# A hybrid diffusion layer on one core: four edits to the order of small steps (norm banks, down weights, output weights' low parts, state copy)

## The chip, the core and the metric

The kernel runs on one core of a Trainium2 chip: TensorE (PE) for matrix products into PSUM, VectorE (DVE), ScalarE (ACT) and GpSimd (POOL) for everything elementwise, SyncE (SP) for issuing most DMAs. Each engine works through its own instructions in order; semaphores tie them together. The metric is the device time of one execution in microseconds, the median of several.

## The reference

One layer over 1024 latent and 128 context tokens with d = 1024, in float32. Cut to what matters here:

```
h   = rmsnorm(x) * (1 + sc1) + sh1
o   = concat(diff_attention, RG-LRU, 2-D Fourier)(h @ w_in) @ w_out     # also new_k, new_v, new_h
x   = x + g1 * rmsnorm(o)
h   = rmsnorm(x) * (1 + sc2) + sh2
gt, up = split(h @ w_gate_up)                                            # hidden 2816
x   = x + g2 * rmsnorm((silu(gt) * up) @ w_down)
```

Attention has 4 heads, each with two score maps whose softmaxes are subtracted; a unit of work below is one head and one tile of 128 queries. new_h are the last states of the LRU.

## The kernel before

**Split products.** Every large product is made of three matmuls: each operand has a high part (fp32r, made by ScalarE) and a low part (operand minus high part, made by VectorE, `lo`, line 174). `mm3` (lines 184 to 186) issues them.

**Order.** The program is one hand-written sequence. Each engine executes its instructions in the order in which this sequence issues them. The LRU, rope, Fourier and modulation work is written as generators in queues; `tick` advances a modelled clock and lets each queue issue its next steps when the modelled time is due. `drain_lru` ticks until the four LRU queues are empty. The last steps of `lru_outs` transpose the four final states (`nht`), copy them (`lw<-nht`) and store them. The PSUM bank `nht` is the one that the next value tile takes.

**Attention.** The loop over n runs through 32 units (and 7 more steps to finish). Step n issues scores of unit n, transposes of unit n-3, products with the values of unit n-4, and the last transpose and scaling of unit n-6 (`finish_hi` on ScalarE, `finish_lo` on VectorE, which writes `mxl`). The softmax weights of unit n-1 are made by VectorE when n mod 3 = 0 and by GpSimd otherwise. The transposed weights have one PSUM bank, which `finish_lo` reads last in a step. Spread over these steps the output projection's weights are read from HBM in eight pieces (`load_wo`, two buffers `wor`), and their high (`woh`) and low parts (`wol`) are made in halves. The high parts are issued at n = 5, 7, 8, 10, 11, 13, ... (n mod 3 = 2 and 1), the low parts at n = 6, 7, 9, 10, 12, 13, ... (n mod 3 = 0 and 1).

**Output projection and second norm.** It runs over 9 token tiles. A finished tile is normed, transposed into two banks of the pool `dn` (`h2_turn`) and scaled (`h2_mod`, lines 1417 on ScalarE or 1420 on VectorE), and split into operands for the gate product. Tile 8 is transposed and scaled only after the gate products have begun.

**Gate products.** Seven products per weight visit g (Strassen-like, `PRODS`), numbered q; the operands of weight q are prepared four products ahead (`prep`). The first three visits use one token chunk only, while `second_chunk` prepares the operands of the other. Product results take PSUM banks in turn: number `nbank` modulo the length of the list `banks`, which has 4 entries, 6 from q = 4 on, and 8 after the transposed tile 8 has been taken. Entries 6 and 7 are the two banks of `dn`.

**Down projection.** 18 runs: column half n = 0 over the 9 tiles, then half n = 1 backwards. A run has 22 steps j of three matmuls. In the first run the down weights arrive: `load_d` reads 512 KB into one of three stages, `split_d(j + 10)` makes high and low part of one 512-column piece, and the second piece of a stage asks for the load three on. The hidden tile of a run is read back from HBM in two halves (`load_h`, two buffers `hr`) and split (`split_h`). `grow` copies a scale row to all partitions (`G2`); `post` uses it after each run.

Of the kernel before, what the change touches and what calls it, by code (L numbers as in the profile page):

```python
# [152 lines left out]
def _body(tc, nc, A):  # L153
# [465 lines left out]
    def lru_outs(f, lw, nh):  # L619
        for u in range(2):  # L620
            yield from until(("scan", u, 0), ("scan", u, 1))
            yield 2.021
            h, h1 = lru["scan", u, 0][0], lru["scan", u, 1][0]
            o = lru["scan", u, 1][1]
            POOL.tensor_tensor(h, h, h1, op=OP.add)
            yield 2.64
            for s0, o0, w in ((0, 0, NL), (NL + GAP, NL, NP)):
                DVE.tensor_tensor(o[:, o0:o0 + w], h[:, s0:s0 + w], ggr[u][:, o0:o0 + w],
                                  op=OP.mult)
            yield 0.994  # L630
            full = ([f.tile([P, TL], F32R, name=f"mo{i}", tag=i, bufs=2) for i in "ri"] if u else None)
            yield from store_mix(f, 4 + u, o, 4, full)
            lru["out", u] = True
        yield from until(*[("fin", u, d) for u in range(2) for d in range(2)])
        b = aux("nht", "a")
        PE.transpose(b[0:4, 0:P], nh.rearrange("p d u -> p (d u)"), ident)
        nhs = lw[0:4, 0, 0, 0]
        copy(ACT, nhs, b[0:4, 0:P])
        SP.dma_start(A["new_h"].rearrange("d (u p) -> (d u) p", p=P), nhs)
# [582 lines left out]
    for n in range(N + 7):  # L1222
        a, t_, v, c = n, n - 3, n - 4, n - 6
        if n == LEAD:
            play("v99")
            wp.release()
            hp.release()
            ax.release()
            wo = pool("wo")
            woh = wo.tile([P, KT, D], F32R, name="woh")  # L1230
            wol = wo.tile([P, KT, D], F32R, name="wol")
            mx = pool("mx")
            al = pool("al")
            tp = pool("tp", bufs=1, space=PSUM, side="right")
            G1 = mx.tile([P, D], F32, name="G1")
            ovec = mx.tile([P, NT, 4], F32, name="ovec")
            grow(G1, 0, 0)
        if n == N - 2:
            load_mix(0, ((4, KT), (0, 3)))
        if n == N + 1:  # L1240
            load_mix(0, ((3, 4),))
            load_x1in(0)
        if n == N:
            sc.release()
            dn = pool("dnps", bufs=2, space=PSUM)
            op = [pool(f"op{i}", space=PSUM) for i in range(2)]
        if has(a):
            U[a] = {}
            h, t = units[a]
            if t == 4 and h + 1 < NH:  # L1250
                load_head(h + 1)
            if t % 3 == 2 or t == 7:
                nx = 3 * h + t // 3 + 2
                if nx < 12:
                    load_q(nx // 3, nx % 3)
            if 3 <= n < 27 and n % 3 == 0:
                load_wo(n // 3 - 1)
            scores(a, 0)
            play(MID.get((n, 0), ""))
        on_dve = n % 3 == 0  # L1260
        if has(t_):
            tgroup(t_, 0, ACT)
        if has(v - 1):
            osquare(v - 1)
            oscale1(v - 1)
        if has(a):
            expo(a, 0)
        if 5 <= n < 29 and n % 3 != 0:
            split_wo((n - 5) // 3, 0 if n % 3 == 2 else 1)
        if has(v):  # L1270
            pv(v, 0)
        if N < n < N + 7:
            next(opg)
        if has(a):
            scores(a, 1, (0, 1))
            play(MID.get((n, 1), ""))
        if has(t_):
            tgroup(t_, 1, DVE)
        if 6 <= n < 30 and n % 3 != 2:
            split_wo_lo((n - 6) // 3, 0 if n % 3 == 0 else 1)  # L1280
        if has(n - 1):
            coef(n - 1)
            if not on_dve:
                weights(n - 1, POOL)
        if has(a):
            scores(a, 1, (1, 3))
            play(MID.get((n, 2), ""))
        if has(v):
            pv(v, 1)
        if has(t_):  # L1290
            bt = tgroup(t_, 2, ACT, c if has(c) else None)
        elif has(c):
            bt = tp.tile([P, 512], F32, name=f"tl{n}", tag="tp")
            PE.transpose(bt[:, CW:], U[c]["on"], ident)
        if has(c):
            finish_hi(c, bt[:, CW:])
        if has(v):
            pv(v, 2)
        if has(v):
            ocopy(v)  # L1300
        if N < n < N + 7:
            next(opg)
        if has(a):
            expo(a, 1)
        if has(c):
            finish_lo(c, bt[:, CW:])
        if has(v - 1):
            oscale2(v - 1)
        if has(n - 1) and on_dve:
            weights(n - 1, DVE)  # L1310
        if has(a) and units[a][1] == 6 and units[a][0] + 1 < NH:
            cache_hi(units[a][0] + 1)
        if has(a) and units[a][1] == 6 and units[a][0] + 1 < NH:
            cache_lo(units[a][0] + 1)
# [92 lines left out]
    def h2_mod(t, q):  # L1407

        r = 0 if t < 8 else 1
        if q == 0:  # L1410
            hu[t] = mo.tile([P, 4, 4, 64], F32, name=f"ou{t}", tag="ou", bufs=2)
        u, b = hu[t], hb.pop((t, q))
        for i in range(4):
            k = 4 * q + i
            o, x = u[:, 2 * q:2 * q + 2, i], b[:, i * P:(i + 1) * P].rearrange("p (h c) -> p h c", h=2)
            if t == 8 or q == HQ:
                ACT.activation(o, x, AF.Identity, scale=S2[:, r, k:k + 1],  # L1417
                               bias=M[:, r, 24 + k:25 + k])
            else:
                DVE.tensor_scalar(o, x, S2[:, r, k:k + 1], M[:, r, 24 + k:25 + k],  # L1420
                                  op0=OP.mult, op1=OP.add)
# [188 lines left out]
    H8 = 4  # L1610
    for v, (g, cs) in enumerate(VIS):
        last = v == NV_ - 1
        for c_ in ([(c,) for c in cs] if last else [cs]):
            if last and c_ == (1,):
                avp.release()
                dp = pool("dp", side="right", reuse_waits="tile")
                load_h(0, 0)
                G2 = [dp.tile([P, D], F32, name="G2"), raw[0][:, 1]]
                fv = dp.tile([P, NT, 2], F32, name="fv")
            for p in range(7):  # L1620
                q = 7 * v + p
                while nprep <= q + LEADQ:
                    prep(nprep)
                    nprep += 1
                if q == 4:
                    op[0].release()
                    gb = pool("gb", space=PSUM, reuse_waits="tile")
                    banks += [4, 5]
                bs = [product(q, c) for c in c_]
                if q in (H8, H8 + 1):  # L1630
                    h2_turn(8, q - H8)
                    h2_mod(8, q - H8)
                if q == H8 + 1:
                    banks += [6, 7]
                after(q, c_, bs)
                if extra is not None and next(extra, 1):
                    extra = None
                if v == NV_ - 2 and p == 3:
                    load_d(0)
                    load_d(1)  # L1640
                if last and c_ == (0,):
                    if p == 0:
                        dw += [mo.tile([P, 2, 512], F32R, name=f"dw{i}", tag="tm" if i < 2 else "ou",
                                       bufs=2) for i in range(4)] + slots
                    if p == 3:
                        load_d(2)
                    if 1 <= p <= 4:
                        split_d(p - 1)
                elif last:
                    if p == 1:  # L1650
                        load_h(0, 1)
                    if p == 4:
                        split_h(0, 0)
                    if p > 0:
                        split_d(p + 3)
# [30 lines left out]
    for i, (n, t) in enumerate(runs):  # L1686
# [6 lines left out]
        for j in range(NJ):  # L1693
            if i == 0 and j + 10 < NJ:
                split_d(j + 10)
            if j == 0:
                if i == 0:
                    grow(G2[0], 1, 0)
                    grow(G2[1], 1, 1)
                if nxt is not None:  # L1700
                    load_h(nxt, 0)
                    load_h(nxt, 1)
                if n:
                    load_x1(t)
            if i == 0 and j == 2:
                split_h(0, 1)
            if nxt is not None and j in ((14, 18) if i == 0 else (8, 14)):
                split_h(nxt, int(j > 8 if i else j > 14))
            if j == 1 and done is not None:
# [40 lines left out]
```

## Time and profile before

| | |
|---|---|
| three runs | 1446.28, 1448.0, 1450.58 us; median 1448.0 |
| profiled execution | 1453.06 us, its span 1451.3 us |
| TensorE busy | 1383.9 us, 95% of the span |
| VectorE, ScalarE, GpSimd busy | 822.7, 572.3, 426.6 us |
| stages in the span, about | scores and values 362 to 545, output projection to 656, gate products to 1160, down projection to the end |

Busy TensorE time contains matmuls whose ends are modelled. A row of waits names the waiting instruction by its engine, output and line and then the instruction that ended the wait. In names, the tile on the left of the arrow is written.

### The profile page before, as it was taken

The page shows a single profiled execution, that of the slowest core. Times are in us where ns is not written, and L with a number is a line of the kernel's source. Part 1 is how long each engine was busy: PE and PEld are TensorE (multiplying, and loading weights), DVE is VectorE, ACT ScalarE, POOL GpSimd, SP SyncE. Part 2 cuts the span into 40 slices and gives each one's busy share as a digit, 9 for nine tenths or more (in the row PEclk, how much of TensorE's full clock was granted, in tenths as well). Part 3 has the DMA queues.
Part 4 walks back from the last instruction along what each step waited for, and adds up shares of the span by engine and source line. Part 5 has one row for each costly group of instructions (what it writes and reads, how often), then busy time and mean ns, then how long its engine had stood idle before and what let it go on. Part 6 is the DMA issues. An engine that isn't in the chain of part 4 may idle for free.

```text
span 1451.3 us, 22745 instructions
## 1 busy us (share of the span) xinstructions
PE 1383.9 (95%) x8918; PEld 1256.6 (87%) x8918; DVE 822.7 (57%) x1251; ACT 572.3 (39%) x1134; POOL 426.6 (29%) x426
## 2 busy tenths in 40 slices
PE   7899999998998899998999999999999989999998
PEld 6787789897888888888899999999999968888886
DVE  5624454664777763676876767667666652233322
ACT  6511236734777773545422323323222342232111
POOL 2301111222565561446643423343324000000000
PEclk9999999999999999999999999999999999999999
DMA  8467750147744425562321322212222472324541
GB/s 311 148 238 257 254 178 30 62 159 169 171 122 121 116 68 175 174 216 101 116 68 71 99 75 92 82 62 85 73 91 78 137 270 82 106 99 172 181 160 58
DMA packets 108326, 193.39 MB, mean 133 GB/s; under 512 B 7702, under 2 KB 77755, under 8 KB 104763
## 3 DMA queue, kind: packets, MB, share of 16 engines
q1 hardware_dynamic: 108074, 191.41, 41.0%
q8 instruction: 70, 1.15, 0.3%
q10 hardware_dynamic: 144, 0.52, 0.1%
q14 instruction: 38, 0.30, 0.1%
HBM read 146.67 MB, written 45.24 MB: 132 GB/s over the span
## 4 chain that ended last, share of the span: by engine, by line
PE 51%; DMA 1%; DVE 1%; ACT 1%; POOL 0%; issue 0%; SPq 0%; DVEq 0%; POOLq 0%; ACTq 0%
PE g L184 11%; PE g L186 11%; PE g L185 11%; PE d L184 6%; PE d L185 6%; PE d L186 6%; DMA raw_gu<-in_w_down 1%; DMA hr<-HB 0%; DVE gu L174 0%; ACT gu L168 0%; DVE hd L174 0%; DVE dw L174 0%; POOL t L1353 0%; ACT ou L1417 0%; ACT hd L168 0%
## 5 line engine op out<-in xcount | busy, mean ns | idle before, releaser
L184 PE MATMUL g<-av,gu 128*128 128x320 f32 (+1 forms) x1232 | 365.6, 297 | 5.5 <-ACT ou L1417 5.5
L186 PE MATMUL g<-av,gu 128*128 128x320 f32 (+1 forms) x1232 | 364.9, 296 | 3.2 <-DVE gu L174 3.2
L185 PE MATMUL g<-av,gu 128*128 128x320 f32 (+1 forms) x1232 | 364.7, 296 | 0.0
L184 PEld LDWEIGHTS g<-av,gu 128*128 128x128 f32 x1232 | 233.4, 189 | 5.7 <-ACT ou L1417 5.7
L186 PEld LDWEIGHTS g<-av,gu 128*128 128x128 f32 x1232 | 233.5, 190 | 3.8 <-DVE gu L174 3.7
L185 PEld LDWEIGHTS g<-av,gu 128*128 128x128 f32 x1232 | 233.7, 190 | 0.0
L174 DVE TENSOR_TENSOR gu<-raw_gu,gu 128x512 fp32r<-128x512 f32 x139 | 141.1, 1022 | 40.1 <-ACT gu L168 40.1
L184 PE MATMUL pu<-hl,w 128*128 128x384 f32 x336 | 124.0, 369 | 4.6 <-POOL hl L174 3.8
L186 PE MATMUL pu<-hh,w 128*128 128x384 f32 x336 | 114.5, 341 | 0.0
L185 PE MATMUL pu<-hh,w 128*128 128x384 f32 x336 | 114.4, 341 | 0.0
L184 PE MATMUL d<-dw,hd 128*128 128x512 f32 x270 | 107.6, 399 | 6.8 <-DVE dw L174 6.8
L185 PE MATMUL d<-dw,hd 128*128 128x512 f32 x270 | 107.3, 398 | 0.0
L186 PE MATMUL d<-dw,hd 128*128 128x512 f32 x270 | 107.2, 397 | 0.0
L1370 POOL TENSOR_TENSOR raw_gu<-raw_gu,t 128x512 f32<-128x512 f32 x25 | 33.2, 1327 | 233.9 <-DVE gu L174 233.9
L939 PE MATMUL s<-ks,qs 128*128 128x384 f32 x384 | 91.6, 360 | 4.3 <-DMA ks<-KL 2.4
L1529 DVE TENSOR_TENSOR u<-g,u 128x320 f32<-128x320 f32 (+1 forms) x176 | 77.4, 450 | 29.8 <-PE g L186 29.8
L952 ACT ACTIVATE p<-s,nm 128x1152 f32<-128x1152 f32 x64 | 78.3, 1224 | 39.0 <-DVE nm L945 28.4
L945 DVE TENSOR_REDUCE nm<-s 128x1 f32<-128x1152 f32 x64 | 86.5, 1352 | 7.6 <-PE s L939 7.3
L1671 ACT ACTIVATE t<-d 128x512 f32<-128x512 f32 x18 | 10.7, 597 | 189.6 <-PE d L186 189.6
L168 ACT ACTIVATE gu<-raw_gu 128x512 fp32r<-128x512 f32 x139 | 83.4, 620 | 3.3 <-DMA raw_gu<-in_w_down 1.7
L1079 POOL TENSOR_SCALAR fv<-fv 128x1 f32<-128x1 f32 x9 | 2.7, 300 | 275.8 <-ACT t L1671 275.8
L184 PEld LDWEIGHTS pu<-hl,w 128*128 128x128 f32 x336 | 64.3, 191 | 21.6 <-issue 14.0
(276 smaller groups left out, 2868.8 us busy)
## 6 DMA issues: line engine op xcount, KB each, us to landing
raw_gu<-in_w_gu SPq DMA_DIRECT2D x25, 1024.0 KB, 4.8
hr<-HB SPq DMA_DIRECT2D x32, 704.0 KB, 4.7
wmb<-in_w_mod SPq DMA_DIRECT2D x32, 512.0 KB, 5.0
raw_gu<-in_w_down SPq DMA_DIRECT2D x22, 512.0 KB, 4.4
HB<-hf SPq DMA_DIRECT2D x18, 576.0 KB, 3.1
x<-in_x SPq DMA_DIRECT2D x18, 512.0 KB, 4.8
wm<-in_w_mod SPq DMA_DIRECT2D x16, 512.0 KB, 8.6
raw<-in_w_in_u SPq DMA_DIRECT2D x14, 512.0 KB, 7.7
```

The lines of the kernel that those rows point to most:

```text
L168: ACT.activation(out, in_, AF.Copy)
L174: eng.tensor_tensor(out, x, hi.bitcast(F32), op=OP.subtract)
L184: PE.matmul(out, wh, xl, start=first, stop=False)
L185: PE.matmul(out, wh, xh, start=False, stop=False)
L186: PE.matmul(out, wl, xh, start=False, stop=last)
L939: PE.matmul(b[:, j, :CW], q[:, st_, m, i * P:(i + 1) * P], ks[:, m, j * CW:(j + 1) * CW], start=(st_ == 0), stop=(st_ == 1))
L945: DVE.tensor_reduce(nm, s, axis=AX.XY, op=OP.max, negate=True)
L952: ACT.activation(p.rearrange("p (n c) -> p n c", c=CW), s, AF.Exp, bias=nm, accum_out=ss)
L1079: POOL.tensor_scalar(v[:, 0:1], v[:, 0:1], v[:, 1:2], D * EPS, op0=OP.add, op1=OP.add)
L1370: POOL.tensor_tensor(b21, b21, t2, op=OP.subtract)
L1529: add = lambda out, x: DVE.tensor_tensor(out, b, x, op=OP.add)
L1671: ACT.activation(t2, b, AF.Square, accum_out=fv[:, t, n:n + 1])
```

## The change

Five places move; none adds or removes work. (1) In `lru_outs` the state transpose is followed by a modelled delay of 4 us before the copy and the store. (2) Low parts of the output weights are issued one step later: at n = 7, 8, 10, 11, ... (n mod 3 = 1 and 2). (3) All eight scalings of tile 7 in `h2_mod` go to ScalarE (so far four of them to VectorE). (4) The list of banks gets its entries 6 and 7 at q = 13 and no longer at q = 5. (5) In the first run of the down projection the two scale rows are issued at step 11 and no longer at step 0, the next run's hidden halves at steps 6 and 8 and no longer at step 0.

```diff
@@ lru_outs
         PE.transpose(b[0:4, 0:P], nh.rearrange("p d u -> p (d u)"), ident)
+        yield 4.0
         nhs = lw[0:4, 0, 0, 0]
@@ attention loop
-        if 6 <= n < 30 and n % 3 != 2:
-            split_wo_lo((n - 6) // 3, 0 if n % 3 == 0 else 1)
+        if 7 <= n < 31 and n % 3 != 0:
+            split_wo_lo((n - 7) // 3, 0 if n % 3 == 1 else 1)
@@ h2_mod
-            if t == 8 or q == HQ:
+            if t > 6 or q == HQ:
@@ gate products
-                if q == H8 + 1:
+                if q == 13:
                     banks += [6, 7]
@@ down projection
             if j == 0:
-                if i == 0:
-                    grow(G2[0], 1, 0)
-                    grow(G2[1], 1, 1)
-                if nxt is not None:
+                if nxt is not None and i:
                     load_h(nxt, 0)
                     load_h(nxt, 1)
                 if n:
                     load_x1(t)
             if i == 0 and j == 2:
                 split_h(0, 1)
+            if i == 0 and j in (6, 8):
+                load_h(nxt, int(j > 6))
+            if i == 0 and j == 11:
+                grow(G2[0], 1, 0)
+                grow(G2[1], 1, 1)
```

## Rows read from the trace of the kernel before

**Rows 1.** Waits of TensorE: waiter, releaser: us in total, times, longest.

```profile
PE t L978 <- DVE mxl L1039: 11.0, 11, 1.6
PE d L184 <- DVE dw L174: 6.8, 2, 6.3
...
PE g L184 <- ACT ou L1417: 5.5, 1, 5.5
...
PE v L184 <- ACT lw L168: 3.2, 1, 3.2
PE g L186 <- DVE gu L174: 3.2, 2, 3.0
```

**Rows 2.** Waits of VectorE in the attention stretch, 370 to 545 us.

```profile
DVE wol L174 <- ACT woh L168: 11.5, 8, 1.4
```

**Rows 3.** Timeline of VectorE, attention: start, us, instruction, [idle before, releaser].

```profile
461.43 0.69 DVE L174 TENSOR_TENSOR wol<-wor,woh 128x512 fp32r<-128x512 f32 x1 [1.43 <-ACT woh L168]
...
463.63 0.34 DVE L1039 SCALAR_TENSOR_TENSOR mxl<-t,gsub,mxh 128x128 fp32r<-128x128 f32 x1
...
466.37 0.56 DVE L170 COPY th<-t 128x384 f32<-128x384 f32 x1 [1.13 <-PE t L978]
...
479.25 0.69 DVE L174 TENSOR_TENSOR wol<-wor,woh 128x512 fp32r<-128x512 f32 x1 [1.43 <-ACT woh L168]
```

**Rows 4.** Timeline of TensorE, attention.

```profile
464.03 0.55 PE L978 MATMUL t<-ident,wt 128*128 128x128 f32 x3 [1.18 <-DVE mxl L1039]
```

**Rows 5.** Timeline of ScalarE, attention.

```profile
466.61 1.22 ACT L952 ACTIVATE p<-s,nm 128x1152 f32<-128x1152 f32 x1 [0.59 <-POOL wt L971]
```

**Rows 6.** Timeline of VectorE, first gate products.

```profile
673.22 1.75 DVE L174 TENSOR_TENSOR gu<-t,gu 128x512 fp32r<-128x512 f32 x1
...
699.54 3.44 DVE L174 TENSOR_TENSOR gu<-raw_gu,gu 128x512 fp32r<-128x512 f32 x2
```

**Rows 7.** Timeline of SyncE: value tiles and states, then output weights.

```profile
318.94 0.90 SPq L877 DMA_DIRECT2D VS<-nk  x2
...
320.93 0.31 SPq L639 DMA_DIRECT2D out_new_h<-lw  x1
...
487.83 0.54 SPq L914 DMA_DIRECT2D wor<-in_w_out  x1
```

**Rows 8.** Timeline of ScalarE, last norm and first gate products.

```profile
659.74 0.63 ACT L1097 ACTIVATE tm<-x 128x512 f32<-128x512 f32 x1 [0.89 <-DVE x L1096]
...
672.25 0.63 ACT L168 ACTIVATE gu<-t 128x512 fp32r<-128x512 f32 x1 [1.45 <-POOL t L1353]
672.78 1.49 ACT L1417 ACTIVATE ou<-ot,M,S 128x128 f32<-128x128 f32 x4
```

**Rows 9.** Windows: us; busy us (instructions) by engine; granted clock, DMA share, GB/s.

```profile
671.74:678.56 6.82, 4.24 (x16) 4.24 (x17) 5.76 (x7) 5.70 (x15) 4.73 (x4) 0.50 0.01 2
...
1176.92:1183.70 6.78, 5.26 (x12) 4.13 (x13) 5.51 (x8) 5.98 (x8) 0.00 (x0) 0.50 0.62 213
```

**Rows 10.** Timeline of SyncE, first down run.

```profile
1164.74 0.44 SPq L1065 DMA_DIRECT2D G<-GR  x1
...
1165.70 2.28 SPq L1600 DMA_DIRECT2D hr<-HB  x2
1168.02 13.77 SPq L1585 DMA_DIRECT2D raw_gu<-in_w_down  x6
```

**Rows 11.** Single DMA issues at 1160.8 and 1168.0: KB, us to landing.

```profile
raw_gu<-in_w_down SPq DMA_DIRECT2D x1, 512.0 KB, 3.3
...
raw_gu<-in_w_down SPq DMA_DIRECT2D x1, 512.0 KB, 9.0
```

**Rows 12.** Timeline of VectorE, first down run.

```profile
1164.81 1.29 DVE L174 TENSOR_TENSOR dw<-raw_gu,dw 128x512 fp32r<-128x512 f32 x2
1166.01 1.62 DVE L174 TENSOR_TENSOR hd<-hr,hd 128x1408 fp32r<-128x1408 f32 x1
```

**Rows 13.** DMA issues over the whole span: count, KB, median us to landing.

```profile
hr<-HB SPq DMA_DIRECT2D x32, 704.0 KB, 4.7
```

## The prediction

> **What bounds the kernel now.** The table above has TensorE busy for nearly the whole span, so I read first which waits of TensorE are left, and what stands behind each. The list of its waits has the longest single ones, and the largest sum, where three of the edits are [rows 1]: 11.0 us in eleven pieces for `mxl`, VectorE's low part of the attention output; 6.8 us in two pieces for a low part of down weights; one piece of 5.5 us for ScalarE's line 1417 (the last tile's second norm) ahead of gate product 6; one of 3.2 us for the copy of the LRU states. The last row, 3.2 us with one piece of 3.0 for a gate weight's low part, is touched by no edit and matters all the same. Then I read each place in the timelines of all engines, to see whether the wait is the bound there or only what happens to come last.
>
> **Low parts of the output weights.** In the units with n mod 3 = 1, VectorE is asked for the low part of the very half whose high part ScalarE makes in the same unit. It stands still for 1.43 us, eight times, 11.5 us in all [rows 2, 3]. Queued behind the waiting instruction are the unit's coefficient, its second row maximum and `mxl` (463.63), which frees the one bank for transposed weights; TensorE then begins its transposes at 464.03 after 1.18 us of waiting [rows 3, 4]. Eight such pieces, the longest of them 1.6, are 8 x 1.2 + 0.4 = 10.0 of the 11.0 us [rows 1].
> With the edit the low part in this unit is that of a half whose high part is two units old, and the other half's low part goes to the unit with n mod 3 = 2, a unit after its high part. The 1.43 us go; 0.69 us of work moves from n mod 3 = 0 to 2. What hides it there: VectorE idles 1.13 us before its copy at 466.37 in that unit, which comes earlier by the same shift [rows 3]. What is late next: ScalarE's exponential at 466.61 waits for GpSimd's weights [rows 5]; GpSimd begins these with the coefficient that stood behind the 1.43 us, so this moves forward with the rest. Gain 10.0 us. Bounds: 11.5, and 1.5 if the moved work is slowed.
> The subtraction of this shape takes 0.69 us here, and 1.75 us at 673.22, where GpSimd works beside it [rows 3, 6]. [...] I take 0.69, since the low part at 461.43 already lies in such a unit and takes 0.69.
>
> **The states' copy.** The 3.2 us for `lw` are real, but the edit only adds a delay to a list worked off by a modelled clock. On SyncE the store of the last value tile is the second at 318.94, and the states' store follows it at 320.93 [rows 7]: these steps are issued by the final draining loop, in which no other list has anything left. Four more ticks put no instruction between transpose and copy. Cost 0. Bounds, should something move: 3.2 us gained, or 4.0 (the modelled delay) lost.
>
> **The last norm and its banks.** Today product 6 goes to a bank that holds the transposed last tile, which ScalarE empties from 672.78 on (four instructions, 1.49 us); ScalarE had been held for 1.45 us by GpSimd's weight sum [rows 8]. With the edit product 6 has a bank long empty, and the wait of 5.5 us goes. But the products behind it need their weights' low parts, and these come from a chain in which TensorE has no part: high part on ScalarE, low part on VectorE, sums on GpSimd, and between them the second token chunk's operands. Product 8 needs the low part that starts at 673.22 and ends at 674.97; product 18 needs the first of the two that start at 699.54 (3.44 us for both), at about 701.3 [rows 6], and this is the piece of 3.0 us in [rows 1]. TensorE ends product 5 at 668.8 (678.56 less 4.24 us busy [rows 9] less 5.5). From there to product 18 are 12.3 products of twelve matmuls; at half clock 16 took 4.24 us, so 0.132 each at full clock, 1.6 us a product, 1.8 with some margin: 22 us of work in 32.5. Without the bank wait TensorE meets the weights' low parts earlier, waits in more and smaller pieces, and leaves at 701.3 as before. Gain 0. Under the same cover lies a new wait: with six banks until product 13 and eight after it, products 16 and 17 get the banks of 12 and 13, whose sums are late. The four norm instructions of tile 7 that go from VectorE to ScalarE are the 1.49 us of above; ScalarE's next one waits 0.89 us for VectorE anyway (659.74) [rows 8], so 0, at most 0.6.
> Bounds: 7.6 us gained (5.5, and 2.1 for 4.24 us at a granted clock of 0.50 [rows 9]), and 6 lost (rival D).
>
> **The first down tile.** The ninth of its eleven weight loads is asked for at 1168.02 and lands 9.0 us later; one with nothing in flight lands after 3.3 [rows 10, 11]. On SyncE it stands behind two scale rows (1164.74, each 512 KB) and two reloads of a hidden tile (1165.70, each 704 KB), the second of which waits for the low part that ends at 1166.01 + 1.62 [rows 10, 12]. Its own buffer was free at 1164.81 + 1.29 = 1166.1 [rows 12]. With the edit it leaves at 1166.1 with one weight load ahead: I take a landing at 1169.5 to 1171. From landing to matmul took 1.4 us (1177.0; 1183.70 less 5.26 busy [rows 9]). So it is ready at 1170.9 to 1172.4, and TensorE, without its first wait of 0.5, wants it at 1171.6. The last pieces follow at the pace of their low parts; I allow 1.1 us of waiting in all. Of 6.8 us of waits and 2.6 of half clock (5.26 us busy at 0.50 [rows 9]), together 9.4, 8.3 go.
> What is late next: the hidden tile with which the second run begins. Its reload now goes out behind the sixth step's load, by my estimate at 1170.2 (the eighth load lands at 1167.9, its high and low parts take 1.9). It lands 4.7 later by the page's median [rows 13], at 1174.9; a high and a low part of at most 1.62 each [rows 12] end at 1178.1. The second run wants it at 1171.6 + 6 x 0.7 + 1.1 = 1176.9. That gives back 1.2 us. The scale rows, asked for at about 1176, are needed only by the first run's norm, whose bank is not wanted for eight runs: 0. Gain 8.3 - 1.2 = 7.1. Bounds: 9.4, and 0.2 where the reload takes 9.0 us (5.5 of waiting and 2.6 of half clock).
>
> **Sum.** The profiled execution took 1453.1 us, 5.1 above the median: 1453.1 - 10.0 - 0 - 0 - 7.1 = 1436.0. From the median of 1448.0 it is 1430.9; I say 1431. Behind each of the places TensorE has no wait of this size left, so the gain should reach the end.
>
> **Rivals.**
> A. The bank wait is worth its price, since the weight chain shortens with it: 1431 - 7.6 = 1423. For it: it is the second longest wait. Against: no link of the chain waits for TensorE. 0.10.
> B. The low parts meet GpSimd, and 1.25 us a period shrink to 1.25 - 1.06 = 0.19: 1.5 us for eight, 1439.5. For it the 1.75 us at 673.22, against it the 0.69 at 461.43 [rows 3, 6]. 0.12.
> C. The reload takes the weight load's place as the late transfer: 0.2 gained there, 1438. For it the 9.0 us, against it that the scale rows now lie behind it. 0.10.
> D. The gate stretch, its idle time cut small, runs at the lower clock throughout: 12.3 x 12 x 0.265 = 39 us in place of 32.5, 1437. Half clock did follow the 5.5 us wait [rows 9]. [...] 0.04.
> E. Slower. A piece of output weights is asked for only when the low part of the piece two before has freed its buffer, and SyncE, which works in order, holds the loads of queries and heads behind that request. Now the buffer is free at 479.25 + 0.69 and the request leaves at 487.83 [rows 3, 7]: 7.9 us of slack, of which the edit uses one unit, 17.82 / 3 = 5.9 (461.43 to 479.25 are three units). Past 7.9 each us would count for six pieces; from a slip of 10.8 on the 17.1 us are undone. A slip of two units, 11.9: 1431 + 6 x 4.0 = 1455. 0.03.
> The forecast keeps 0.61, with a range of its own of 1426 to 1436.
>
> **Numbers.** 1422 to 1440 takes in the cases A to D. About 0.3%, 4.3 us, is what a measurement of this kernel can tell from no change. Slower than that: E and a little for mishaps, 0.04. Within it: B and C together, 0.06. Faster: 0.90.
>
> **What would show it.** Right: `wol` no longer waits for `woh`; TensorE's row for `mxl` falls from 11.0 to between 1 and 3 us; no wait for line 1417, but several smaller ones for gate low parts, with product 18 some 32 us behind product 5 as before; no 6.3 us wait in the first down tile, and one of about 1 us for `hd` ahead of the second; the 3.2 us at the states' copy unchanged. Wrong: low parts that take 1 us or more, a wait of ScalarE for `wor`, a second run that waits several us for `hd`, or product 18 well before 32 us.

## The result and the profile after

The changed kernel took 1432.6 us in the median of four runs (1430.3 to 1439.2) beside 1449.3 for the kernel before in the same comparison: a ratio of 0.9892, interval 0.985 to 0.9934, 15.7 us. Its profiled execution took 1430.3 us, with a span of 1428.5. Timed again later (the run "changed, again" below, with a profile of its own, here called the second profile) it took 1433.05 against 1452.14: 0.9869, 0.9852 to 0.9885, 19.0 us.

TensorE's waits after the change (waiter, releaser: us in total, times, longest), answering to [rows 1]:

```profile
PE g L186 <- DVE gu L174: 7.3, 6, 2.2
...
PE v L184 <- ACT lw L168: 3.5, 1, 3.5
PE d L184 <- DVE dw L174: 3.1, 2, 1.9
...
PE t L979 <- DVE mxl L1040: 1.1, 3, 0.6
...
PE d L186 <- DVE hd L174: 0.9, 1, 0.9
PE g L184 <- ACT av L168: 0.8, 1, 0.8
```

The row for `mxl` has fallen from 11.0 to 1.1, and that for line 1417 (5.5) is gone. In its place the gate's low parts have grown from 3.2 to 7.3 in six pieces. The wait at the states' copy is as it was. In the first down tile 6.8 us have become 3.1, and a new 0.9 for the hidden tile stands ahead of the second run.

VectorE in the attention after the change, answering to [rows 3]. These are the low parts in the units with n mod 3 = 1 of two successive periods of three units (start, us, instruction, [idle before]):

```profile
447.92 0.68 DVE L174 TENSOR_TENSOR wol<-wor,woh 128x512 fp32r<-128x512 f32 x1
...
464.16 0.68 DVE L174 TENSOR_TENSOR wol<-wor,woh 128x512 fp32r<-128x512 f32 x1
```

No idle time stands before them, and a period is 16.24 us long; before it was 17.82 [rows 3].

Where the time went, by stage. Each stage runs from its first matmul in TensorE's timeline to that of the next stage, the last one to the last matmul; us:

| kernel | ahead of the scores | attention | output projection | gate | down |
|---|---|---|---|---|---|
| before | 342.5 | 198.8 | 115.8 | 503.1 | 284.7 |
| changed | 338.2 | 185.1 | 115.8 | 502.8 | 280.1 |
| changed, again | 336.6 | 185.7 | 115.8 | 502.8 | 281.4 |
| low parts only | 343.4 | 185.1 | 115.8 | 503.1 | 284.2 |
| banks only | 342.7 | 197.5 | 115.8 | 503.1 | 285.0 |
| down only | 343.0 | 198.0 | 115.8 | 503.1 | 279.3 |
| scales only | 341.7 | 197.5 | 115.8 | 503.1 | 281.9 |
| reloads only | 342.0 | 197.8 | 115.8 | 504.1 | 280.8 |
| low parts apart | 344.4 | 185.8 | 115.8 | 504.1 | 279.3 |
| gate two thirds | 341.5 | 185.0 | 115.8 | 503.0 | 281.5 |
| fourth stage | 340.9 | 186.4 | 115.8 | 503.1 | 279.0 |
| no token sums | 341.4 | 186.0 | 115.8 | 502.3 | 279.5 |
| all three | 345.3 | 185.2 | 115.8 | 502.8 | 278.5 |
| apart and stage | 343.1 | 185.0 | 115.8 | 502.8 | 278.6 |

Rows with "only" are the kernel before with a part of the change, those below them the changed kernel with something more or less; each is one profile. The first column is to be read first. All kernels but "all three" have the same order of instructions up to the scores, and still it runs from 336.6 to 344.4. So the 4.3 us by which the two profiled executions differ there are no effect of the change. From the scores on, the changed kernel is 18.6 us shorter than the kernel before: 13.7 in the attention, 0.3 in the gate stage and 4.5 in the down stage; its second profile is 16.6 us shorter. Single profiles scatter by 1 to 2 us in the attention and in the down stage: the attention takes 197.5 to 198.8 us in the five profiles with the old order of low parts and 185.0 to 186.4 in the nine with a new one, 12.4 apart in the mean.

### The profile page after: what moved, and what is told of

Its sections match the earlier page's. It is cut to its first block, busy times and chain, and to the rows that moved or that the text cites. A ratio compares the mean times of both kernels' runs of the same rounds, so it can differ in the third digit from the quotient of the medians.

```text
span 1428.5 us, 22758 instructions
## 1 busy us (share of the span) xinstructions
PE 1375.9 (96%) x8918; PEld 1248.9 (87%) x8918; DVE 822.0 (58%) x1247; ACT 573.4 (40%) x1138; POOL 427.6 (30%) x426
## 4 chain that ended last, share of the span: by engine, by line
PE 49%; DVE 2%; issue 1%; ACT 1%; DMA 1%; POOL 0%; DVEq 0%; POOLq 0%; SPq 0%; ACTq 0%
PE g L186 10%; PE g L184 10%; PE g L185 10%; PE d L186 6%; PE d L184 6%; PE d L185 6%; DVE gu L174 1%; DMA hr<-HB 1%; DVE av L174 0%; ACT gu L168 0%; DMA raw_gu<-in_w_down 0%; DVE u L1530 0%; DVE hf L1530 0%; DVE hd L174 0%; ACT av L168 0%
## 5 line engine op out<-in xcount | busy, mean ns | idle before, releaser
L1672 ACT ACTIVATE t<-d 128x512 f32<-128x512 f32 x18 | 10.7, 596 | 186.4 <-PE d L186 186.4
```

The source lines that it names most:

```text
L1672: ACT.activation(t2, b, AF.Square, accum_out=fv[:, t, n:n + 1])
```

## The experiments

**The three parts alone.** Each is the kernel before with one part of the change, the lines as in the diff above: the low parts; the banks with the scalings of tile 7; the scale rows with the reloads.

> The kernel before with only the output weights' low parts one step later. By the prediction's term it is 10.0 us shorter than the kernel before. By the stage in the two traces, where the units with n mod 3 = 2 fell from 7.0 to 5.6 us from scores to scores and all 24 units from 362 on gained 13.7 us with 1.5 of it at unit 0 that the change doesn't touch, it is about 12 us shorter. If the gain of the attention came from elsewhere (a different clock, a shift in the transfers), it is less than 8. In the trace VectorE's wait of the low parts for the high parts (11.5 us in eight pieces) should be gone, and TensorE's wait for mxl 1 to 2 us.

> The kernel before with only the banks given to gate products from product 13 on and tile 7's scalings on ScalarE. My theory: the weights' low parts are the bound there, so no gain, within 2 us of the kernel before, the wait for ScalarE's line 1417 replaced by 6 to 8 us of waits for gate low parts, and product 18 again some 32 us behind product 5. Rival: the bank wait is worth its price and the whole gate stage is 5.5 to 7.6 us shorter.

> The kernel before with only the scale rows and hidden reloads of the first down run moved. By the prediction's term 7.1 us shorter; by the down stage of the two traces (284.3 against 279.7 us from the first matmul to the last) 4.5 us shorter, with waits of 3 us for down weights and 1 us for the hidden tile left. Rival: nothing (under 1 us), since the reload is late instead.

Beside 1451.7 us for the kernel before, the low parts alone took 1438.8 (ratio 0.9911, 0.9888 to 0.9934: 12.9 us), the banks alone 1451.9 (1.000, 0.9983 to 1.0016) and the down part alone 1445.8 (0.9959, 0.9941 to 0.9977: 6.0 us). The parts sum to 18.9 us, and the change as a whole measured 15.7 and 19.0. For the low parts the estimate from the stage (12) came nearer than the prediction's term (10.0), though the interval (9.6 to 16.3 us) holds both. The theory of no gain at the banks holds. The down part gave 5.4 us in the stage of its profile, between the two figures expected (7.1 and 4.5).

The gate stage is read from two rows of TensorE's timeline per kernel: the first gate matmul, and the first matmul of product 18 that uses its weight's low part. Before:

```profile
657.06 0.39 PE L184 MATMUL g<-av,gu 128*128 128x320 f32 x1
...
701.34 0.41 PE L186 MATMUL g<-av,gu 128*128 128x320 f32 x1 [2.97 <-DVE gu L174]
```

The kernel with the banks alone:

```profile
656.00 0.39 PE L184 MATMUL g<-av,gu 128*128 128x320 f32 x1
...
700.32 0.41 PE L186 MATMUL g<-av,gu 128*128 128x320 f32 x1 [2.21 <-DVE gu L174]
```

44.28 and 44.32 us. With the bank wait TensorE stood once for 5.5 us and once for 3.0; without it, it stands for 6.8 us in five pieces for low parts and reaches product 18 at the same distance. Of the fourteen profiles eight have 44.3 us here, and five, with the old banks and with the new, 45.2 to 45.3 (the one left has 45.0, below); what makes this difference of 1 us is open.

**The low parts apart.** The moved low parts also leave a unit in which VectorE makes the softmax weights (n mod 3 = 0). Was that a part of the gain?

```diff
-        if 7 <= n < 31 and n % 3 != 0:
-            split_wo_lo((n - 7) // 3, 0 if n % 3 == 1 else 1)
+        if 6 <= n < 30 and n % 3 == 0:
+            split_wo_lo((n - 6) // 3, 0)
+        if 8 <= n < 32 and n % 3 == 2:
+            split_wo_lo((n - 8) // 3, 1)
```

> The changed kernel, but each first half's low part back in the units with n mod 3 = 0, where it was before the change, and each second half's in the units with n mod 3 = 2. No low part then stands behind a high part of its own unit, and none lies in a unit with n mod 3 = 1. If the gain of the attention is the removed wait alone, the stage is as long as in the changed kernel (185 us from the first scores to the output projection, within 1). If a part of it came from work leaving the units in which VectorE also makes the softmax weights (n mod 3 = 0), the stage is 2 us or more longer than that.

The attention took 185.8 us against 185.1 and 185.7 in the two profiles of the changed kernel: the gain comes from the removed wait, and within 1 us it doesn't matter which of the other units takes the work. The kernel took 1431.2 us (0.9862, 0.9838 to 0.9886), which can't be told from the changed kernel.

**The two halves of the down part.**

> The kernel before with only the two scale rows of the first down run moved to step 11, the hidden reloads left at step 0. My theory is that both the rows and the reloads stand on SyncE ahead of the ninth weight load, and that the second reload's wait for its buffer is what holds the load back: the load then still leaves at about 2 us after its buffer is free, lands after 5 to 6 us in place of 9, and 2 to 4 us are gained. Rival: the two rows of 512 KB were all of it, and the gain is that of the whole part (4.5).

> The kernel before with only the hidden reloads of the first down run moved to steps 6 and 8, the scale rows left at step 0. By my theory the ninth load leaves on time but shares the transfers with 1 MB of scale rows: 2 to 4 us gained. Rival: the order on SyncE was all of it, and the gain is that of the whole part (4.5).

The scale rows alone gave 0.9978 (0.9961 to 0.9996), 3.2 us; the reloads alone 0.9969 (0.9949 to 0.9989), 4.5 us. By the stage it is 2.8 and 3.8, where both together have 5.4. The wait for weights in the first down run (6.8 before) is, in this order, with the scale rows moved, with the reloads moved, and with both:

```profile
PE d L184 <- DVE dw L174: 4.6, 1, 4.6
```

```profile
PE d L184 <- DVE dw L174: 3.7, 1, 3.7
```

```profile
PE d L184 <- DVE dw L174: 2.1, 2, 1.5
```

Each half does part of it and neither all, so both theories hold and both rivals fall. The ninth weight load, on SyncE and by its landing, shows what each does. Before, it leaves 7.9 us after the first down matmul and lands 9.0 us later. With the scale rows moved it leaves at 7.9 as before and takes 6.5; with the reloads moved it leaves at 5.4 and takes 8.5; with both, 5.1 and 6.2. So the reloads hold the request back on SyncE, and the scale rows, under way with it, lengthen its landing.

**Is TensorE the bound in the gate stretch?** One matmul in three is left out of products 6 to 17:

```diff
+            if 6 <= q < 18:
+                PE.matmul(b, w[:, 0, ks], al_[:, a, k, :n], start=k == 0, stop=False)
+                PE.matmul(b, w[:, 1, ks], ah[:, a, k, :n], start=False, stop=k == 3)
+                continue
             mm3(b, w[:, 0, ks], w[:, 1, ks], ah[:, a, k, :n], al_[:, a, k, :n], k == 0, k == 3)
```

> The changed kernel with one of three matmuls (high part by high part) left out of gate products 6 to 17, so the result is another. TensorE then has some 6 us less to do between product 5 and product 18. If the chain of weights is the bound there, product 18 still comes some 32 us behind product 5, TensorE's waits in that stretch grow by 5 to 6 us, and the kernel is within 1.5 us of the changed kernel. If TensorE itself is the bound behind its bank waits, product 18 comes 5 to 6 us earlier and the kernel is that much shorter.

The same two rows of this kernel:

```profile
642.33 0.39 PE L184 MATMUL g<-av,gu 128*128 128x320 f32 x1
...
687.53 0.42 PE L186 MATMUL g<-av,gu 128*128 128x320 f32 x1 [1.57 <-DVE gu L174]
```

45.20 us: with a third of its matmuls gone TensorE is no earlier, and the stage is as long as ever (503.0). The kernel took 1435.0 us in one run. The chain of weights is the bound here, shown. One expectation was missed: TensorE's waits in the stretch grew from 8.0 to 10.8 us and not by 5 to 6. The granted clock was 0.85 there, where the two profiles of the changed kernel have 1.00 and 0.96, so TensorE was busy for 34.2 us where it had been for 36 to 37.

**What is the chain bound by?** The token sums of `second_chunk` are left out:

```diff
             token_operands1(AV[1], hu[t], t - PT[0])
-            token_sums(hu[t])
             yield
```

> The changed kernel without GpSimd's token sums for the second token chunk (lines 1390 to 1393, four sums for each of four tiles, left out, so the result is another). So far product 18 came 44.3 us after the first gate product whatever the banks did. My theory is that VectorE's chain of low parts is the bound there and that GpSimd working beside it stretches the low parts (1.04 us in the mean for 128x512 from SBUF, in place of 0.69). Without the sums the low parts should average under 0.95 us, and product 18 should come 3 to 7 us earlier. Rival: the chain is bound by its order or by GpSimd's weight sums alone, and product 18 still comes within 1 us of 44.3.

VectorE's costliest group from 640 to 690 us (busy us, mean ns | idle before), first in the changed kernel, then in this one:

```profile
L174 DVE TENSOR_TENSOR gu<-raw_gu,gu 128x512 fp32r<-128x512 f32 x14 | 14.4, 1041 | 4.5 <-ACT gu L168 4.5
```

```profile
L174 DVE TENSOR_TENSOR gu<-raw_gu,gu 128x512 fp32r<-128x512 f32 x13 | 13.0, 1013 | 3.4 <-ACT gu L168 3.4
```

The low parts still take 1.01 us in the mean, and product 18 comes at 688.18 - 643.21 = 44.97 us. My theory falls: without these sums the chain is no shorter. But the mean mixes two kinds of low part. In the changed kernel sixteen low parts of weights begin between the first product and product 18. Those that began more than 0.1 us into a sum of GpSimd took 0.83 to 1.77 us, and each ended about 0.55 us after that sum. The others took 0.68 to 0.69, but for one of 1.26 that began within 0.1 us of a sum's start; another such took 0.68. Without the token sums GpSimd makes its weight sums earlier, and these do the same to a low part at the start of the stage. GpSimd and VectorE in this kernel:

```profile
651.68 1.44 POOL L1355 TENSOR_TENSOR raw_gu<-raw_gu 128x512 f32<-128x512 f32 x1
```

```profile
651.92 1.74 DVE L174 TENSOR_TENSOR gu<-raw_gu,gu 128x512 fp32r<-128x512 f32 x1
```

In the changed kernel that low part took 0.68 us (at 645.83). TensorE waits 2.9 us for it in product 4, and from product 14 on the products come as late as in the changed kernel (32.6 us after the first in both). So GpSimd's sums do stretch the low parts, the weight sums as well as the token sums; which link sets the end of the chain stays open.

**A fourth stage for the down weights, and what lies beyond.**

```diff
-            r = (raw[1][:, 0], raw[1][:, 1], raw[0][:, 0])[i % 3]
+            r = (raw[1][:, 0], raw[1][:, 1], raw[0][:, 0], raw[0][:, 1])[i % 4 if i < 8 else i % 8 % 3 if i < 11 else (i - 8) % 3]
...
-                load_d(i // 2 + 3)
+                if i // 2 != 7:
+                    load_d(i // 2 + (4 if i // 2 < 7 else 3))
...
                     if p == 3:
                         load_d(2)
+                        load_d(3)
```

> The changed kernel with a fourth stage for the down weights: the place of the second scale row holds the fourth and the eighth weight load until step 5, so that each of the loads 4 to 11 can leave one load earlier. If the remaining 3.1 us of TensorE's waits for down weights are a matter of loads that leave too late (three in flight at most), they fall under 1 us and the kernel is 2 to 3.5 us shorter than the changed kernel. If the transfers themselves are at their limit there, the loads take longer instead and nothing is gained (within 1).

It took 1433.4 us (0.9877, 0.9849 to 0.9905). Its wait for weights was 1.6 us, where under 1 was expected, and its down stage 279.0. The two kernels below that also have the fourth stage wait 0.7 and 0.9 us and have 278.5 and 278.6. The six profiles with the whole down part and three stages have waits of 1.4 to 3.2 and down stages of 279.3 to 281.5. So by the stage it gains 1.5 us in the mean, less than the expected 2 to 3.5; the time of the kernel can't tell it from nothing.

The run "all three" adds the low parts apart to this, and moves the states' steps out of `lru_outs` to a place further on, behind more of the value tiles:

```diff
...
     play(before)
+    lw, nh = lru["nht"]
+    b = aux_free("nht")
+    PE.transpose(b[0:4, 0:P], nh.rearrange("p d u -> p (d u)"), ident)
+    nhs = lw[0:4, 0, 0, 0]
+    copy(ACT, nhs, b[0:4, 0:P])
+    SP.dma_start(A["new_h"].rearrange("d (u p) -> (d u) p", p=P), nhs)
     P_["lru"].release()
```

> The changed kernel once more, timed beside the next one. By the sum of the three parts run alone (12.9, 0 and 5.9 us) it is 19 us shorter than the kernel before, by the first comparison 16.7.

> The changed kernel with three things more: the low parts apart (first halves in units with n mod 3 = 0, second halves with n mod 3 = 2), the fourth stage of down weights, and the states' transpose, copy and store moved behind the next 36 steps of the value tiles. By the stages of the runs so far the first is worth 1 us in the attention, the second 0.3 to 1.1 in the down stage, and the third should turn the wait of 3.5 us for the copy into 1 to 2: 2.5 to 4 us shorter than the changed kernel. Rival: the value tiles then meet the copy elsewhere, or the order of the transfers after it shifts, and it is within 1.5 us of the changed kernel.

> The run with all three without its third part: the changed kernel with the low parts apart and the fourth stage of down weights, the states' copy where the changed kernel has it. From the first scores on the run with all three was 3.5 us shorter than the changed kernel; ahead of them it waited 4.4 us for two transfers of queries and keys each. If those waits came from the states' store behind the other transfers, this kernel keeps the 2.5 to 3.5 us and is 1429 to 1431 us, with waits for queries of about 1 us again. If they come from run to run, its time stays at that of the run with all three, 1434 to 1436.

In this order they took 1433.05, 1435.7 (0.9882, 0.9868 to 0.9897) and 1431.8 us (beside 1454.1 before: 0.9847, 0.9828 to 0.9866). The run with all three was expected 2.5 to 4 us below the changed kernel, or within 1.5 of it; it came out 2.6 above. TensorE's waits from 300 to 350 us, first in the second profile of the changed kernel, then with the states' steps later:

```profile
PE v L184 <- ACT lw L168: 4.1, 1, 4.1
PE s L940 <- DMA ks<-KL: 2.8, 1, 2.8
...
PE sp L1143 <- DMA qp<-QHP: 0.9, 1, 0.9
```

```profile
PE sp L1138 <- DMA qp<-QLP: 4.4, 1, 4.4
PE s L935 <- DMA ks<-KL: 4.4, 1, 4.4
PE sp L1138 <- DMA qp<-QHP: 0.8, 1, 0.8
```

The wait for the copy is gone, and in its place TensorE waits 4.4 us for the prompt's queries, whose loads don't come earlier: the copy's wait had hidden theirs. Then `ks` is late too. SyncE's timeline with the states' steps later, the store and the load behind it:

```profile
333.31 0.29 SPq L1217 DMA_DIRECT2D out_new_h<-lw  x1
...
336.91 0.60 SPq L164 DMA_DIRECT2D ks<-KL  x1
```

In the second profile of the changed kernel:

```profile
314.83 0.31 SPq L640 DMA_DIRECT2D out_new_h<-lw  x1
...
326.86 0.61 SPq L164 DMA_DIRECT2D ks<-KL  x1
```

The store now leaves 18.5 us later. On SyncE it stands directly ahead of the loads of `qs` and `ks`, which leave 10 us later. Without this part the first waits are back and the time falls to 1431.8; from the scores on that kernel is 1.6 and 3.6 us shorter than the two profiles of the changed kernel. Its ratio and that of the changed kernel overlap, so it is the shortest ratio measured but not shown to be faster than the change.

## Why the prediction came out

**Sum.** 17.1 us were predicted off the median, 1431; measured were 15.7 and 19.0. The mechanisms are right, but that the sum comes so near is in part luck: two terms were mis-sized in opposite directions, the low parts by 2.6 us too little and the down tile by 1.7 to 3.9 too much.

**Low parts: mechanism right, term too small.** 10.0 us were predicted, with 11.5 as the bound. The two periods above differ by 17.82 - 16.24 = 1.58 us, eight times 12.6, which is past that bound; the run with the low parts alone gave 12.9. What failed is the step "eight such pieces ... are 8 x 1.2 + 0.4". It took idle time for lost time. TensorE's scores in such a unit of the kernel before, ahead of the transposes of [rows 4]:

```profile
461.53 1.32 PE L939 MATMUL s<-ks,qs 128*128 128x384 f32 x6
...
468.56 1.32 PE L939 MATMUL s<-ks,qs 128*128 128x384 f32 x6
```

The transposes follow at 464.03, 2.50 us after the scores began. After the change:

```profile
449.46 1.31 PE L940 MATMUL s<-ks,qs 128*128 128x384 f32 x6
450.60 0.49 PE L979 MATMUL t<-ident,wt 128*128 128x128 f32 x3
...
455.04 1.32 PE L940 MATMUL s<-ks,qs 128*128 128x384 f32 x6
```

1.14 us. So 1.36 us were lost where the row says 1.18: idle time begins at the modelled end of the scores, and a matmul that follows without a wait starts before that end (450.60 is less than 449.46 + 1.31). That accounts for 8 x 0.18 = 1.4 us of the 2.6 missing. From scores to scores this unit fell from 7.03 to 5.58 us, 0.09 more than the 1.36. The unit ahead of it, which gave up a low part, fell by 0.13 (5.40 to 5.27), and the third stayed at 5.4.

Rival B is out; all sixteen low parts of the changed kernel (ns min/median/max):

```profile
L174 DVE TENSOR_TENSOR wol<-wor,woh x16: 680/681/694, 380.9 to 504.3; 128x512 fp32r<-128x512 f32 x16
```

The prediction was right to take 0.69, but it argued from the unit (one in which GpSimd makes the softmax weights), and it is the moment that counts. GpSimd around the low part at 447.92:

```profile
447.43 0.55 POOL L180 TENSOR_TENSOR so<-so,mhalf 128x1 f32<-128x1 f32 x1
...
449.11 1.22 POOL L971 TENSOR_SCALAR wt<-p,c 128x1152 f32<-128x1152 f32 x1 [1.12 <-PE t L982]
```

GpSimd makes the softmax weights from the coefficient `c`, which VectorE makes behind the low part, so they can't begin before it is over (here they wait a little longer, for TensorE); beside the sixteen low parts GpSimd had nothing under way but instructions of 128x1. In the gate stretch of the same kernel it is otherwise. GpSimd and VectorE:

```profile
654.34 2.25 POOL L1355 TENSOR_TENSOR raw_gu<-raw_gu 128x512 f32<-128x512 f32 x1
```

```profile
655.38 1.75 DVE L174 TENSOR_TENSOR gu<-t,gu 128x512 fp32r<-128x512 f32 x1
```

The same form of subtraction took 1.75 us here, beside a sum of 128x512, and 0.68 at 645.83, where GpSimd was idle. Rival B's price of 1.06 us a piece is 1.75 - 0.69 [rows 3, 6]; no run shows it for a moved low part, since all sixteen took 0.68 to 0.69. A low part moved beside the softmax weights themselves might have met that price; no run here tries it.

Rival E is out too: the attention as a whole got shorter by more than the term, so no slip of the loads is in it.

**Banks: right.** 0 predicted, ratio 1.000 measured. Product 18 followed 44.3 us after the first product before and after (32.9 after the end of product 5, where 32.5 was read), and a third fewer matmuls for TensorE did not bring it forward. That rules out rival A, and with it D: TensorE's pace is not what counts here. D's slower clock throughout did not come either: no run shows its 0.265 us a matmul for the whole stretch. From the first product to product 18, in the first and in the second profile of the changed kernel (window, its length, busy us of TensorE, its weight loads, VectorE, ScalarE and GpSimd, granted clock, DMA share and GB/s):

```profile
639.15:683.43 44.28, 36.11 (x229) 32.86 (x228) 34.17 (x47) 26.53 (x58) 31.17 (x28) 1.00 0.34 122
```

```profile
638.21:682.48 44.27, 37.17 (x230) 34.38 (x228) 34.17 (x47) 26.53 (x58) 31.15 (x28) 0.96 0.35 122
```

In the first the granted clock was 1.00 in each 10 us from 640 to 710, through nine pieces of waiting, the longest of 2.2 us; in the second it was 0.96 over the stretch. TensorE was busy for 36.1 and 37.2 of 44.3 us. What sets the clock is not shown. ScalarE's four more scalings cost nothing that the stage shows.

**States' copy: right.** The order of transpose and copy is unchanged, and so is the wait (3.5, 4.1 and 4.0 us where it was 3.2).

**Down: mechanism right, term too large.** 7.1 us were predicted; the stage gave 5.4 in the part alone, and 4.5 and 3.2 in the two profiles of the change. From start to start in TensorE's timeline, the difference lies in the first two of the 18 runs; the next fifteen take 15.27 or 15.28 us each in all these profiles, and the last is as long in all. Before, the first run took 24.96 us, 9.7 above that; the prediction had 6.8 + 2.6 = 9.4. In the part alone it took 18.27, and 19.10 and 20.40 in the change: 3.0, 3.8 and 5.1 us are left, where the prediction allowed 1.1. The hidden tile made the second run 1.3 us longer (1.2 predicted; the row of waits has 0.9). The 2.6 us for the clock came back in full in the first profile of the change and only in part in the second, where the granted clock was 0.92 and the longest wait for weights 1.9 us; the first down run in both:

```profile
1141.93:1161.03 19.10, 15.91 (x69) 11.96 (x67) 12.02 (x20) 10.91 (x17) 0.74 (x1) 1.00 0.76 249
```

```profile
1140.97:1161.37 20.40, 18.02 (x68) 12.78 (x66) 12.83 (x21) 10.92 (x17) 0.74 (x1) 0.92 0.73 240
```

What failed is the allowance of 1.1 us for the weights: TensorE's idle time for them was 2.1 to 3.1, and the waits again cost more than their idle time (3.0 us for 2.1 in the part alone, 3.8 for 3.1 in the change). The step behind it is the landing of the ninth load, "1169.5 to 1171", or 3.4 to 4.9 us after it leaves. SyncE in the changed kernel, and the issue at 1147.06 (KB, us to landing):

```profile
1145.85 6.52 SPq L1586 DMA_DIRECT2D raw_gu<-in_w_down  x4
1152.43 0.42 SPq L1601 DMA_DIRECT2D hr<-HB  x1
...
1160.23 0.43 SPq L1066 DMA_DIRECT2D G<-GR  x1
```

```profile
raw_gu<-in_w_down SPq DMA_DIRECT2D x1, 512.0 KB, 6.5
```

The load leaves ahead of reloads and scale rows, as predicted, but 1.2 us behind another of 512 KB, and takes 6.5. Rival C is out: the hidden tile cost 1.3 us, not 5.5.

## What to carry to other kernels

Price a removed wait from start to start of the instructions around it, with a place in the same loop that has no wait as the measure; the idle time in a row of waits was too low here, 1.18 for 1.36 us and 0.9 for 1.3. Before removing a long wait, ask which chain delivers the data of the next products, and whether that chain contains the waiting engine: at the banks and at the states' copy it did not, and most of the waiting or all of it came back a few instructions later (6.8 us where 5.5 and 3.0 had been, 4.4 where 4.1 had). A load freed from its queue still lands later beside other loads (6.2 to 6.5 us behind one of its size, 3.3 for the one that the prediction took as alone), so price it by a load in company. And price an instruction beside another engine by what that engine has under way at that moment (1.75 and 0.68 us for one form of subtraction here), not by the stretch of the program that both lie in.

## What was not expected of the hardware

The granted clock differs between executions of one kernel with the same instructions: 1.00 and 0.96 in the gate stretch of the two profiles of the changed kernel, 1.00 and 0.92 in their first down run, with 3.1 and 2.3 us of waits for weights there. The gate stage is no longer for it (502.8 in both), since TensorE is not the bound there; the first down run is longer by 1.3 us. And the stretch ahead of the scores varies by 8 us between executions with the same order of instructions, as much as half of this change.
